# Hybrid attention block: where ScalarE's and VectorE's queued casts stand within a step

## The chip, the cores and the metric

One core of one Trainium2 chip runs the whole program. The metric is the device time of one execution in microseconds, the median over several runs. The work is shared by TensorE (PE, with its weight loads PEld), VectorE (DVE), ScalarE (ACT), GpSimd (POOL) and the DMA queue that SyncE (SP) issues to.

## What is computed

One layer over 1024 tokens of width 1024. Group A is neighbourhood attention on a 16 x 64 grid, group B windowed attention with rotary positions and a sink logit. Both have eight heads of 64 (group B two heads for keys and values).

```python
h = jnp.einsum('bsd,de->bse', x, w_in[layer])
q_a, k_a, v_a, z_a, q_b, k_b, v_b, z_b = jnp.split(h, SPLIT_POINTS, axis=-1)
y_a = neighborhood_attention(q_a, k_a, v_a, rel_pos_bias[layer])
y_b = windowed_gqa_with_sink(rotary(q_b), rotary(k_b), v_b, sink_logits[layer])
mixed = jnp.concatenate([y_a * jax.nn.silu(z_a), y_b * jax.nn.silu(z_b)], axis=-1)
y = jnp.einsum('bse,ed->bsd', mixed, w_out[layer])
x = layer_norm(DEEPNORM_ALPHA * x + y, ln_gain[layer], ln_bias[layer])
```

(The reshapes into heads are left out here.) The kernel keeps nearly full float32 accuracy by splitting operands into a high and a low float16 part, and multiplying high by high, high by low and low by high.

## The kernel before

The program has three parts. A prologue projects v in float32 and the first six of 21 tiles of 128 columns (`ORDER`, `NPRO`). Then comes a loop over attention units, and last `final()`: the rest of the output projection and the layer norm. The change lies in the loop (lines 1171 to 1240).

A **unit** is one head's block of 128 queries; there are 128 (`unit_list`: 64 of group B, then 64 of group A). At step i the loop issues the score matmuls of unit i (`stage_qk`, L815 and L816, into one of four "s" banks of PSUM), VectorE's fused reduction that adds the bias and finds the maximum (L825), ScalarE's exponential (`stage_exp`, L841), and for unit i-1 the split of the probabilities (`stage_tr`): high part on ScalarE (L851), low part on VectorE (L852), and a transposing DMA on SP (L855). The product with v follows for four units at once, at least six steps later (`stage_pv`, L880). It is then scaled (`stage_on`, L886 and L889), transposed (L900) and multiplied by the gate (L903, L909).

Between the score matmuls the loop fills TensorE with the **projection** of the remaining 15 tiles (`FILL`, `project`, L395), a tile being two halves of the tokens with 24 matmuls of 512 columns each, every half in one of two "pj" banks of PSUM. `FILL_AT` gives the steps over which a tile is spread, about eight for each. `pump_to(i + F1)` issues a first fifth of a step's share and `pump_to(i + 1)`, at the end of the step, the rest. When the 24th matmul is issued, `evac` queues what empties the bank. For k and q that is, for each of two heads on 64 partitions, a cast to the high part on ScalarE (L271, `hi` of `split_hl`) and a subtraction for the low part on VectorE (L277, `lo`). For gates z it is a tanh on ScalarE (L355) and a product on VectorE (L356). For rotary q it is a copy on ScalarE (L325), behind which a shuffle on VectorE and products on GpSimd follow. A bank can be written again only when all its readers are done, and with two banks that is one half (24 matmuls) later.

Each engine executes in the order of issue, which is written out by hand here: `enq` puts such an operation into a list of its engine with a priority (0 for those that hold a bank, 0.5 for weights, 1 for the rest), and `pop(eng, n, top)` issues up to n of those whose predecessors were issued in an earlier step, best priority first. In the loop before, `pop("dve", ...)` stands behind `stage_tr` and `stage_on`, then `stage_exp`, then `pop("act", ...)`, `pop("pool", ...)`, and the rest of the projection's share. So in a step ScalarE's order is L851 of the unit before, L841, queued operations; VectorE's is L825, L852 of the unit before, queued operations. `NA` and `ND` are 1: one queued operation for each engine and step; ScalarE gets two where its list holds five or more, or from step 105 on (`M_AT[0]`), VectorE two from step 112 on. `need` issues an operation at once where the order demands it.

Of the kernel before, what the change touches and what calls it, by code (L numbers as in the profile page):

```python
# [26 lines left out]
LTT, LPP, BP, BH, BR, ND, NA, NX, F1 = 1, 6, 2, 9, 5, 1, 1, 6, 0.2  # L27
# [18 lines left out]
M_AT = [105, 112, 118, 120]  # L46
# [16 lines left out]
def hybrid_block(ctx, tc, xT, x, wt, wv, wo, bias, sink, gain, lbias, cos, sin, bmask, out):  # L63
# [78 lines left out]
    queues = {e: [] for e in ENG}  # L142
    clock = {"step": None}
# [10 lines left out]
    def enq(eng, fn, *deps, prio=1, after=0):  # L154
        op = Op(eng, fn, deps, prio)
        if clock["step"] is not None:
            queues[eng].append(op)
        elif after:
            events.setdefault(ran[0] + after, []).append(op.emit)
        else:  # L160
            op.emit()
        return op

    ran, events = [0], {}

    def pop(eng, n, top=1):
        q = queues[eng]
        ready = [op for op in q if op.prio <= top and all(d.step is not None and d.step + d.lag < clock["step"] for d in op.deps)]
        for op in sorted(ready, key=lambda op: op.prio)[:n]:
            q.remove(op)  # L170
            op.emit()

    def need(*ops):
        for op in ops:
            if op.step is None:
                need(*op.deps)
                queues[op.eng].remove(op)
                op.emit()
# [244 lines left out]
    def wo_scan(n):  # L423
        nc.scalar.activation(scrap[:, :512], wo_raw[n], AF.Abs, accum_out=wom[:, n:n + 1])
# [310 lines left out]
    def gather_v(p, b):  # L735
        w = WINW[b]
        t = ap.tile([128, 4, 256], F16, tag="va", name=f"va{p}_{b}", bufs=6)
        bulk["last"] = bulk["step"]
        nc.sync.dma_start(t[:4 * w], vwin[b][p].rearrange("(g i) (c e) -> (i c) g e", g=4, e=256))
        va[p, b] = t  # L740
# [24 lines left out]
    def geom(u):  # L765
        g, p, j, t, _ = u
        if g == "a":
            b, half = t
            w = WINW[b]
            return NKEY[b], [4 * w] * 3  # L770
        lo, hi = max(t - 1, 0), min(t + 2, 8)
        return 128 * (hi - lo), [128] * (hi - lo)

    def stage_load(u, i):
        g, p, j, t, _ = u
        n, _c = geom(u)
        if g == "a":
            b, half = t
            if half == 0 and b != 2:
                bulk["last"] = clock["step"] + 1  # L780
                bt = ap.tile([128, 23 * WINW[1]], F32, tag="bs", name="bias", bufs=BR)
                o, m = BOFF[b], 23 * WINW[b]
                nc.sync.dma_start(bt[:, :m], bias[2 * p + j, :, o:o + m])
                bv = bt[:, :m]
                ld = Op("sp", None, [], 1)
                ld.step = i
                op = enq("pool", lambda: nc.gpsimd.tensor_scalar(bv, bv, rsg, -1.0, op0=ALU.mult, op1=ALU.mult),  # L787
                         ld, prio=0)
                st["bias"] = bt, op
            o = 11 * WINW[b] * half  # L790
            st[u, "b"] = st["bias"][0][:, o:o + NROW[half] * WINW[b]], st["bias"][1]
# [52 lines left out]
    def stage_tr(u):  # L844
        g, p, j, t, _ = u
        n, ch = geom(u)
        pt = st.pop((u, "p"))
        c, m = ch[0], len(ch)
        hl = split[units.index(u) % NSPLIT]
        src = pt[:, :n].rearrange("p (k c) -> p k c", c=c)  # L850
        nc.scalar.activation(hl[:, :m, 0, :c], src, AF.Copy, scale=PSCALE)  # L851
        nc.vector.scalar_tensor_tensor(hl[:, :m, 1, :c], src, PSCALE, hl[:, :m, 0, :c],  # L852
                                       op0=ALU.mult, op1=ALU.subtract)
        tr = ap.tile([128, 6, 128], F16, tag="tr", name="tr", bufs=BH)
        nc.sync.dma_start(tr[:, :2 * m, :], hl[:, :m].rearrange("p k i c -> p (k i c)"), transpose=True)  # L855
        st[u, "tr"] = tr

    def quad(q):
        g, p, j, t, _ = units[4 * q]
        return g, p, j, t // 4 if g == "b" else t[0] // 2  # L860
# [57 lines left out]
    def pump_to(u):  # L918
        n = 0
        for k, c in enumerate(FILL_N):  # L920
            u0, u1 = FILL_AT[k], FILL_AT[k + 1]
            n += int(c * min(max((u - u0) / (u1 - u0), 0), 1))
        pump(n - pumped[0])
        pumped[0] = max(n, pumped[0])
# [16 lines left out]
    def wo_max():  # L941
        nc.vector.tensor_reduce(wog, wom, axis=mybir.AxisListType.X, op=ALU.max)

    def wo_turn():
        ps = bank("t")
        nc.tensor.transpose(ps[:, :128], wog.to_broadcast([128, 128]), identf)
        wo_parts["max"] = ps
# [12 lines left out]
    def wo_load(n):  # L960
        if n < 16:
            tag = WO_TAG[n]
            pool, bufs = (rawp, 3) if tag == "raw" else (wp, {"wr": 5, "wor": 2}[tag])
            raw = pool.tile([128, 512], F32, tag=tag, name=f"wor{n}", bufs=bufs)
            e, a = WO_SEQ[n]
            nc.sync.dma_start(raw, wo[e, :, 512 * a:512 * a + 512])
            wo_raw[n] = raw
# [37 lines left out]
    def m_queue(e):  # L1005
        m_alloc(e, big)
        m_ops[e] = []
        for h in (slice(0, 512), slice(512, S)):
            o = enq("act", lambda h=h: nc.scalar.copy(mh[e][:, h], zt[e][:, h]))
            m_ops[e].append(enq("pool", lambda h=h: nc.gpsimd.tensor_sub(  # L1010
                ml[e][:, h], zt[e][:, h], mh[e][:, h]), o))
# [159 lines left out]
    for i in range(-LD, NU + LO):  # L1171
        if 0 <= i + LD < NU:
            stage_load(units[i + LD], i)
        if i < 0:
            continue
        clock["step"] = i
        per, h = divmod(i, 16)
        bulk["step"] = i
        if i in VA_AT:
            gather_v(0, VA_AT.index(i))  # L1180
        for n in range(len(WO_LD)):
            if WO_LD[n] == i:
                load_ops["wo", n] = enq("sp", lambda n=n: wo_load(n), wo_ops.get({9: 0, 10: 1, 12: 2, 13: 3}.get(n)),
                                        w_ops.get(17 + n if 4 <= n <= 8 else None))
                if n not in WO_PRE + WO_POST:
                    scan_ops.append(enq("act", lambda n=n: wo_scan(n), load_ops["wo", n]))
        if i == WO_MAX - 6:
            for n in WO_POST:
                scan_ops.append(enq("act", lambda n=n: wo_scan(n), load_ops["wo", n]))
        if i == WO_MAX:  # L1190
            need(*scan_ops)
            wo_max()
        for n in range(len(WO_AT)):
            if WO_AT[n] == i:
                wo_split(n)
        if i == 131:
            enq("sp", gain_load, *m_ops[4])
        if i in M_AT:
            m_queue(4 + M_AT.index(i))
        if bulk["last"] != i or (queues["sp"] and i - queues["sp"][0].born > 2):  # L1200
            pop("sp", 1 if i < 118 else 3)
        if i < NU:
            u = units[i]
            if u[3] in (0, 4):
                need(*stk_ops[f"b{u[1]}", u[2], u[3] // 4])
            if u[3] == (0, 0):
                need(*stk_ops[u[1], u[2], 0], *stk_ops[u[1], u[2], 1])
            stage_qk(u)
        q, m = divmod(i - LP - 3, 4)
        if i >= Q30 + 2:  # L1210
            q, m = (NU // 4 - 2, i - Q30 - 2) if i < Q30 + 4 else divmod(i - LP - 3, 4)
        elif i >= Q30:
            q, m = -1, 0
        if m == 0 and 0 <= q - 1 < NU // 4:
            stage_ot(q - 1)
        if m == 0 and 0 <= q < NU // 4:
            stage_pv(q)
        if i > Z3_END:
            pop("dve", 1, 0)
        if 0 <= i - LT < NU:  # L1220
            stage_tr(units[i - LT])
        if 2 <= i < 10:
            m_scale(i - 2)
        if i == WO_MAX + 3:
            wo_turn()
        if WO_MAX + 4 <= i < WO_MAX + 7:
            wo_scale(i - WO_MAX - 4)
        pump_to(i + F1)
        if 0 <= q < NU // 4:
            g, p, j, h = quad(q)  # L1230
            if g == "a" and p < 3 and (j, h, m) in VA_STEP:
                gather_v(p + 1, VA_STEP.index((j, h, m)))
        if m == 1 and 0 <= q < NU // 4:
            stage_on(q)
        pop("dve", ND if i < M_AT[1] else 2)
        if i < NU:
            stage_exp(units[i])
        pop("act", NA if i < M_AT[0] and len(queues["act"]) < 5 else 2)
        pop("pool", NP)
        pump_to(i + 1)  # L1240
    pump(10 ** 6)
# [77 lines left out]
```

## Time and profile before

| | us |
|---|---|
| median of 3 runs | 454.24 |
| lowest and highest | 451.89, 456.68 |
| the profiled execution | 452.2 |
| its span, first to last instruction | 450.4 |
| TensorE busy | 438.8 |
| VectorE busy | 347.1 |
| ScalarE busy | 300.9 |
| GpSimd busy | 231.9 |

The granted clock of TensorE is 0.994 of full speed over the span. A row of the profile gives line, engine, operation, what is written and read, and a count. In a row of the timeline the first number is the start and the second the time taken, both in us; a bracket says how long the engine stood idle before it and what ended that. In a row of waits stand the total in us, how often, and the longest. The modelled end of a matmul lies behind the start of the next, so that the distance between two starts tells more than a matmul's length.

### The profile page before, as it was taken

Reading aid. Unit: us, or ns where it says so; the run is one execution under the profiler, and the core shown is the slowest. Engines: PE = TensorE matmul, PEld = TensorE weight load, DVE = VectorE, ACT = ScalarE, POOL = GpSimd, SP = SyncE. Lnnn points to the kernel's source line nnn. Section 1 sums busy time; section 2 is a strip of 40 time slices with the busy share of each in tenths; the row PEclk is TensorE's granted clock in tenths of the full one; section 3 lists DMA queues with packets and bytes.
Section 4 is the critical chain, followed back from the end, with each engine's and each line's share of the span. In section 5 each row is a group of like instructions: output and inputs, shape, how many; then the busy total and the mean of one; then the engine's idle time right before and its main releaser. Section 6 shows DMA issues by size and latency. Waiting matters only on the chain.

```text
span 450.4 us, 9544 instructions
## 1 busy us (share of the span) xinstructions
PE 438.8 (97%) x3265; PEld 263.1 (58%) x3265; DVE 347.1 (77%) x860; ACT 300.9 (67%) x702; POOL 231.9 (51%) x246
## 2 busy tenths in 40 slices
PE   9999999999999999999999999999999999999992
PEld 8999974444445555555554565656546654444452
DVE  5878978839978787786788887887777847389954
ACT  5648659867588889888868877888678874012200
POOL 0003943555827849868506729755483547005741
PEclk9999999999999999999999999999999999999997
DMA  8898378977837889777979898989999989101711
GB/s 282 266 309 281 83 249 253 301 259 257 279 109 157 152 174 174 135 152 134 158 159 159 182 184 164 228 149 211 213 181 219 191 168 355 56 0 70 258 71 70
DMA packets 135280, 83.86 MB, mean 186 GB/s; under 512 B 101440, under 2 KB 113600, under 8 KB 134976
## 3 DMA queue, kind: packets, MB, share of 16 engines
q1 hardware_dynamic: 134800, 82.84, 75.3%
q8 instruction: 25, 0.41, 0.4%
q10 hardware_dynamic: 432, 0.43, 0.3%
q14 instruction: 23, 0.19, 0.1%
HBM read 52.83 MB, written 9.96 MB: 139 GB/s over the span
## 4 chain that ended last, share of the span: by engine, by line
PE 75%; DVE 7%; issue 7%; POOL 6%; ACT 3%; DMA 1%; DVEq 0%; SPq 0%; POOLq 0%; ACTq 0%
PE ps_pj L395 28%; PE ps_s L1028 9%; PE ps_t L880 6%; PE ps_s L476 6%; PE ps_pj L1028 5%; PE ps_t L1028 5%; PE ps_s L815 3%; PE ps_s L816 3%; PE ps_pj L476 3%; PE ps_t L476 3%; POOL wl L203 3%; POOL wr L202 2%; PE ps_t L900 2%; DVE split L852 1%; DVE sn L825 1%
## 5 line engine op out<-in xcount | busy, mean ns | idle before, releaser
L395 PE MATMUL ps_pj<-xf,wh 128*128 128x512 f16 x672 | 202.2, 379 | 1.8 <-DVE ks L277 1.1
L395 PE MATMUL ps_pj<-xf,wl 128*128 128x512 f16 x336 | 127.3, 379 | 0.0
L395 PEld LDWEIGHTS <-wh 128*128 128x128 f16 x672 | 63.5, 98 | 62.6 <-DVE ks L277 2.0
L852 DVE SCALAR_TENSOR_TENSOR split<-ps_s,split 128x384 f16<-128x384 f32 (+2 forms) x128 | 65.7, 514 | 33.1 <-ACT split L851 32.4
L841 ACT ACTIVATE ps_s<-sn,nm 128x385 f32<-128x385 f32 (+3 forms) x128 | 70.2, 548 | 29.0 <-DVE nm L825 27.2
L1028 PEld LDWEIGHTS <-m 128*128 128x128 f16 x408 | 39.7, 98 | 41.3
L851 ACT ACTIVATE split<-ps_s 128x384 f16<-128x384 f32 (+2 forms) x128 | 57.4, 448 | 1.8
L395 PEld LDWEIGHTS <-wl 128*128 128x128 f16 x336 | 32.9, 98 | 37.4
L202 POOL TENSOR_SCALAR wr<-wr,wsc 128x512 f32<-128x512 f32 x26 | 21.7, 836 | 42.9 <-ACT wh L197 37.9
L825 DVE CUSTOM_DVE_ANT_0 sn<-ps_s,bias,sg 128x264 f32<-128x264 f32 (+1 forms) x64 | 35.0, 547 | 8.3 <-PE ps_s L816 3.9
L825 DVE CUSTOM_DVE_ANT_0 sn<-ps_s,bm,nsk 128x384 f32<-128x384 f32 (+1 forms) x64 | 40.7, 636 | 0.6 <-PE ps_s L816 0.3
L1028 PE MATMUL ps_s<-wo,m 128*128 128x512 f16 (+1 forms) x192 | 40.7, 366 | 0.0
L815 PE MATMUL ps_s<-ks,qs 128*128 128x384 f16 (+4 forms) x128 | 39.2, 306 | 0.6 <-DVE zg L681 0.3
L816 PE MATMUL ps_s<-ks,qs 128*128 128x384 f16 (+4 forms) x128 | 39.2, 306 | 0.0
L787 POOL TENSOR_SCALAR bias<-bias,rsg 128x552 f32<-128x552 f32 (+1 forms) x24 | 18.6, 777 | 38.3 <-DMA bias<-in_bias 33.1
L880 PEld LDWEIGHTS <-tr 128*128 128x128 f16 (+1 forms) x1104 | 36.6, 98 | 2.2
L203 POOL TENSOR_TENSOR wl<-wr,wh 128x512 f16<-128x512 f32 x26 | 32.2, 1238 | 2.2
L1121 POOL TENSOR_TENSOR xr<-xr,gb 128x512 f32<-128x512 f32 x7 | 11.1, 1598 | 37.2 <-ACT xr L1118 37.2
L476 PE MATMUL ps_s<-wvh,x 128*128 128x320 f32 x128 | 29.5, 310 | 0.0
L309 POOL COPY ks<-ks 64x512 f16<-64x512 f16 x40 | 26.1, 660 | 6.2 <-DVE ks L279 1.8
L1028 PE MATMUL ps_pj<-wo,m 128*128 128x512 f16 (+1 forms) x120 | 26.4, 358 | 0.0
L524 POOL TENSOR_SCALAR xraw<-xraw,xsc 128x512 f32<-128x512 f32 x5 | 4.5, 905 | 39.2 <-ACT xf L522 39.2
(182 smaller groups left out, 826.8 us busy)
## 6 DMA issues: line engine op xcount, KB each, us to landing
xraw<-in_xT SPq DMA_DIRECT2D x31, 256.0 KB, 4.3
ws<-in_wt SPq DMA_DIRECT2D x15, 512.0 KB, 5.3
wr<-in_wt SPq DMA_DIRECT2D x26, 256.0 KB, 3.1
bias<-in_bias SPq DMA_DIRECT2D x16, 276.0 KB, 3.4
wor<-in_wo SPq DMA_DIRECT2D x16, 256.0 KB, 3.3
xr<-in_x SPq DMA_DIRECT2D x8, 512.0 KB, 9.1
out<-xr SPq DMA_DIRECT2D x14, 256.0 KB, 2.1
bias<-in_bias SPq DMA_DIRECT2D x8, 368.0 KB, 3.9
```

Of the source, the lines that this page charges most:

```text
L202: nc.gpsimd.tensor_scalar(raw, raw, scale, 1.0, op0=ALU.mult, op1=ALU.mult)
L203: nc.gpsimd.tensor_sub(l, raw, h)
L395: nc.tensor.matmul(ps, a[:, k % 4, :], mv, start=(k == 0 and i == 0), stop=(k == KT - 1 and i == 2))
L476: nc.tensor.matmul(ps[:, :320], lh[t // 4, k][:, ts], rh[k][:, cs], start=(k == 0 and i == 0), stop=(k == KT - 1 and i == 2))
L815: nc.tensor.matmul(ps[:, :m], q, sl[0], start=True, stop=False)
L816: nc.tensor.matmul(ps[:, :m], q, sl[1], start=False, stop=True)
L825: nc.vector.tensor_tensor_reduce(sn[:, :m], ps[:, :m], bias_t, sg[:, c:c + 1], init, op0=ALU.add, op1=ALU.min, accum_out=nm)
L841: nc.scalar.activation(pt[:, :m], sn[:, :m], AF.Exp, bias=nm, scale=-1.0, accum_out=sm[:, k:k + 1])
L851: nc.scalar.activation(hl[:, :m, 0, :c], src, AF.Copy, scale=PSCALE)
L852: nc.vector.scalar_tensor_tensor(hl[:, :m, 1, :c], src, PSCALE, hl[:, :m, 0, :c], op0=ALU.mult, op1=ALU.subtract)
L880: nc.tensor.matmul(ps[:, HD * m:HD * m + HD], a, b_, start=(i == 0), stop=(i == len(mms) - 1))
L1028: nc.tensor.matmul(ps, lh[:, ts], rh[:, cs], start=(e == EO[0] and i == 0), stop=(e == EO[-1] and i == 2))
```

## The change

Behind `stage_tr`, and so ahead of the exponential, one queued ScalarE operation of priority 0 may be issued; what it takes is subtracted from the step's number behind the exponential. `pop` now returns how many it issued, and takes `late`: with 1, predecessors issued in the same step count as done. If VectorE's list issued nothing in the step, one operation of priority 0 may be issued at the end of the step under that looser rule.

```diff
-    def pop(eng, n, top=1):
+    def pop(eng, n, top=1, late=0):
         q = queues[eng]
-        ready = [op for op in q if op.prio <= top and all(d.step is not None and d.step + d.lag < clock["step"] for d in op.deps)]
-        for op in sorted(ready, key=lambda op: op.prio)[:n]:
+        ready = [op for op in q if op.prio <= top and all(
+            d.step is not None and d.step + d.lag < clock["step"] + late for d in op.deps)]
+        ready = sorted(ready, key=lambda op: op.prio)[:n]
+        for op in ready:
             q.remove(op)
             op.emit()
+        return len(ready)
...
             stage_tr(units[i - LT])
+        early = pop("act", 1, 0)
         if 2 <= i < 10:
...
-        pop("dve", ND if i < M_AT[1] else 2)
+        turned = pop("dve", ND if i < M_AT[1] else 2)
         if i < NU:
             stage_exp(units[i])
-        pop("act", NA if i < M_AT[0] and len(queues["act"]) < 5 else 2)
+        pop("act", (NA if i < M_AT[0] and len(queues["act"]) < 5 else 2) - early)
+        if not turned:
+            pop("dve", 1, 0, 1)
         pop("pool", NP)
```

## The prediction

> **What bounds the kernel now.** I read the page first, then the busy times by stage, the waits of TensorE (its matmuls and its weight loads), the rows of TensorE in order of time, and last the rows of the two engines that the change reorders.
>
> ```profile
> span 450.4 us, 9544 instructions
> PE 438.8 (97%) x3265; PEld 263.1 (58%) x3265; DVE 347.1 (77%) x860; ACT 300.9 (67%) x702; POOL 231.9 (51%) x246
> 124.00:245.00 121.00, 120.35 (x1037) 67.88 (x1036) 97.64 (x290) 101.67 (x262) 74.04 (x76) 1.00 0.78 151
> ```
>
> TensorE is busy for 438.8 of 450.4 us. The third line is a stage of the loop, with the columns PE, PEld, DVE, ACT, POOL, granted clock: TensorE stands still for 0.65 of 121 us, and ScalarE (101.67, 84%) and VectorE (97.64, 81%) are full but not the bound. So an edit that only reorders casts can win no more than what TensorE waits for them. Those waits:
>
> ```profile
> PE ps_pj L395 <- DVE ks L277: 1.1, 1, 1.1
> PE ps_pj L395 <- DVE qs L277: 0.6, 1, 0.6
> PE ps_s L815 <- DVE zg L681: 0.3, 1, 0.3
> PE ps_s L815 <- DVE split L852: 0.2, 1, 0.2
> PEld L395 <- DVE ks L277: 2.0, 3, 1.4
> PEld L395 <- DVE qs L277: 1.2, 2, 0.8
> ACT qs L271 <- DVE qs L277: 5.5, 6, 1.2
> ```
>
> The reader should see that the low part of a k or q cast (L277) is the one thing of this change that TensorE waits for: 1.7 us by the matmuls' idle time, 3.2 us by the weight loads' (the two count the same waits and aren't added). The true loss lies between, because a matmul's modelled end hides part of a gap. It shows in the starts:
>
> ```profile
> 191.03 1.13 PE L880 MATMUL ps_t<-vb,tr 128*128 128x64 f16 x33
> 192.18 0.38 PE L395 MATMUL ps_pj<-xf,wh 128*128 128x512 f16 x1
> ...
> 229.09 1.13 PE L880 MATMUL ps_t<-vb,tr 128*128 128x64 f16 x33
> 230.21 0.38 PE L395 MATMUL ps_pj<-xf,wh 128*128 128x512 f16 x1
> ...
> 237.43 0.38 PE L395 MATMUL ps_pj<-xf,wl 128*128 128x512 f16 x1
> 237.85 0.38 PE L395 MATMUL ps_pj<-xf,wh 128*128 128x512 f16 x1
> ...
> 245.00 0.31 PE L815 MATMUL ps_s<-ks,qs 128*128 128x352 f16 x1
> 245.15 0.31 PE L816 MATMUL ps_s<-ks,qs 128*128 128x352 f16 x1
> 246.54 0.39 PE L395 MATMUL ps_pj<-xf,wh 128*128 128x512 f16 x1 [1.08 <-DVE ks L277]
> ...
> 275.41 1.22 PE L880 MATMUL ps_t<-va,tr 96*128 96x64 f16 x36
> 276.72 0.39 PE L395 MATMUL ps_pj<-xf,wh 128*128 128x512 f16 x1
> ...
> 335.69 0.28 PE L816 MATMUL ps_s<-ks,qs 128*128 128x264 f16 x1
> 336.53 0.39 PE L395 MATMUL ps_pj<-xf,wh 128*128 128x512 f16 x1 [0.56 <-DVE qs L277]
> ```
>
> L815 and L816 are alike, so their distance (0.15 at 245.00) is what such a matmul takes from start to start. From 245.15 the next should start at 245.30 and starts at 246.54: 1.24 lost. At 335.69 a matmul of 264 columns takes 0.11 (0.15 x 264 / 352), so 336.53 is 0.73 late. 512 columns take 0.22, so 237.85 is 0.20 late. The small matmuls L880 run at (1.13 - 0.19) / 32 = 0.03 each (0.19 being the modelled length of one), so 192.18, 230.21 and 276.72 are some 0.18, 0.15 and 0.25 late. **Sum 2.75 us**, between the two bounds.
>
> **The change part by part.** It adds and removes no instruction and no DMA. It moves two kinds: a high part, tanh or rotary copy that is ready (priority 0, L271, L355, L325) from behind the step's exponential (L841) to ahead of it on ScalarE, and the low part or product that follows (L277, L356) from the middle of the next step to the end of its own on VectorE, ahead of the next reduction (L825). One place, that of the largest stall, before the change (VectorE first, then ScalarE):
>
> ```profile
> 241.40 0.56 DVE L852 SCALAR_TENSOR_TENSOR split<-ps_s,split 128x384 f16<-128x384 f32 x1
> 241.87 0.17 DVE L886 RECIPROCAL ri<-sm 128x4 f32<-128x4 f32 x1
> 242.07 0.43 DVE L889 TENSOR_TENSOR on<-ps_t,ri 128x256 f32<-128x256 f32 x1
> 242.41 0.54 DVE L825 CUSTOM_DVE_ANT_0 sn<-ps_s,bm,nsk 128x256 f32<-128x256 f32 x1
> 243.06 0.56 DVE L852 SCALAR_TENSOR_TENSOR split<-ps_s,split 128x384 f16<-128x384 f32 x1
> 243.53 0.67 DVE L277 SCALAR_TENSOR_TENSOR ks<-ps_pj,ks 64x512 f16<-64x512 f32 x1
> 244.17 0.45 DVE L825 CUSTOM_DVE_ANT_0 sn<-ps_s,bias,sg 128x264 f32<-128x264 f32 x1
> 245.33 0.42 DVE L852 SCALAR_TENSOR_TENSOR split<-ps_s,split 128x256 f16<-128x256 f32 x1 [0.70 <-ACT split L851]
> 245.79 0.69 DVE L277 SCALAR_TENSOR_TENSOR ks<-ps_pj,ks 64x512 f16<-64x512 f32 x1
> ```
>
> ```profile
> 240.88 0.49 ACT L851 ACTIVATE split<-ps_s 128x384 f16<-128x384 f32 x1
> 241.47 0.59 ACT L841 ACTIVATE ps_s<-sn,nm 128x385 f32<-128x385 f32 x1
> 242.08 0.57 ACT L271 ACTIVATE ks<-ps_pj 64x512 f16<-64x512 f32 x1
> 242.56 0.47 ACT L851 ACTIVATE split<-ps_s 128x384 f16<-128x384 f32 x1
> 243.00 0.48 ACT L841 ACTIVATE ps_s<-sn,nm 128x257 f32<-128x257 f32 x1
> 244.30 0.59 ACT L271 ACTIVATE ks<-ps_pj 64x512 f16<-64x512 f32 x1 [0.70 <-DVE sn L822]
> 244.92 0.38 ACT L851 ACTIVATE split<-ps_s 128x256 f16<-128x256 f32 x1
> ```
>
> The bank's four readers go one after another: cast 242.08, low part 243.53, cast 244.30 (0.10 behind the low part's end; the profile names the short memset beside it), low part until 246.48, and 0.06 later TensorE starts. The bank's matmuls were issued by 237.43, so for over four us nothing but the order of the queues held the first cast back.
>
> I now lay the same durations in the new order. First cast behind L851: 241.37 to 241.94. (What is new is that the exponential now stands behind the cast's wait for the bank's last matmul; but that matmul stands ahead of the step's own score matmuls on TensorE, which the exponential needs anyway, so this wait costs it nothing.) Exponential 241.94, 0.47 later than before. VectorE ends L889 at 242.50, then takes the first low part until 243.17, then the reduction (242.41 before) until 243.71: **0.76 late**. L851 is ready at 242.65. The next L852 ends at 244.27 instead of 243.62: 0.65 late. The second cast goes behind L851 and the first low part, 243.2 to 243.8, without the wait of 0.70. Its exponential starts at 243.8, 0.8 late. The second low part, behind L852, ends at 244.95 instead of 246.48: **the bank is free 1.5 us earlier**, against a stall of 1.24. After that L851 (0.45 early) and the reduction after next (some 0.6 early) have won back the delay, since the wait of 0.70 on each of the two engines is gone.
>
> What covers the delay of 0.65 on L852: the score matmul four units on reuses its bank. For the L852 that ended at 243.62 that matmul is the one at 245.00, so 1.38 us of cover there, 0.7 left. With the cover gone it would cost up to 0.65 for each such pair of casts. SP's transposes wait for L852 and go as much later:
>
> ```profile
> DMA to landing us min/median/max: 2.4/3.2/5.6
> ```
>
> They land in a median of 3.2 us, and the matmuls that read them (L880) stand at least six steps behind in the program, so 0.65 lies inside that. POOL: copies of k (L309) become ready a step earlier, and have a priority below weights and bias, so nothing is moved behind them. On SP the order of issue stays as it is, since nothing that SP issues hangs on these casts.
>
> The tanh and its product (L355, L356) move in the same way, one pair for a bank. TensorE shows no wait for them: 0. The rotary copies (L325) move 0.6 within a step and have no low part behind them: 0, between -0.1 and +0.1 for each.
>
> Two edges. From step 105 on two ScalarE operations may go in a step: then the second cast stands behind the exponential, ahead of the first low part in the program. If the low part must wait for it, VectorE stands still for about one exponential, the next reduction comes some 0.8 late, and the bank is free about 1 us earlier instead of 1.5. That still covers the stall of 0.73. Also the test for five queued operations now sees one fewer: at exactly five, a cast of weights (L197) or a scan (L424) goes a step later. That is hidden by the eight or so steps for which weights are made ready ahead; a weight load that such a cast releases on SP goes a step later too, with the same cover.
>
> The first of these hangs on who may read a bank together. In the rows (5.5 us over six times in the waits of ScalarE on L277) the second cast waits for the first low part, though one reads partitions 64 to 127 and the other 0 to 63. The Trainium skill (PSUM — Partial Sum Buffer, section "PSUM bank collisions raise a hardware error") says that the compiler orders two engines on one bank, reads against reads too, but by quarters of the partitions, so that these two would be free. The trace differs: here the order goes by the whole bank. By that rule the sum would be the same at 2.75 and the delay of the edge 0 instead of 0.8, hidden either way.
>
> **Sum.** Gain at most 2.75 (the stalls), bounds 1.7 and 3.2. New waits: 0 where the cover holds as at the shown place; I take 0.15 for the first steps, where TensorE waits for the score banks already (0.3 and 0.2 in the waits), upper bound 11 (16 halves of k and q x 0.65). So 450.4 - 2.75 + 0.15 = 447.8 for the span and 449.6 for the profiled run (452.2). That run stands 2.0 under the median of 454.24; from the median the same 2.6 gives 451.6. I take the middle of the two bases, 450.6.
>
> **The rivals.**
> *The gain is lost at another wait* (no change). TensorE is then held up at the score banks or, at the loop's end, by SP, as much as it was at the projection's banks. For it: VectorE runs 81% full in the stage shown. Against it: the new order takes idle time out of both engines. Time: 452.2 on the profile's base, 454.2 on the median's. Chance 0.17.
>
> *The reductions come too late* (slower). Each low part now stands ahead of a reduction, so exponential, L852 and the score bank are late by 0.65 for each pair. Where the cover is smaller than that, TensorE waits. It decides as soon as the cover, 1.38 at the shown place, is under 0.65 at most pairs. 16 x 0.65 = 10.4 less 2.75 is +7.7: 460 to 462; with half of the pairs +2.5: 455 to 457. Against it: in the whole trace TensorE waits for L852 but once, 0.2. Chance 0.10, half of it with all pairs.
>
> *More than the stalls* (the shorter chain also removes the 0.3 and 0.2 at the score banks): 2.75 + 0.5 gives 449.0 to 451.0. Chance 0.08.
>
> **How the numbers follow.** The forecast, stalls gone and nothing new, has 0.65: 449 to 452 by its two bases. The range of 447.5 to 455.5 adds no change and the lighter half of the slower case above, and below the scatter of the runs (451.89 to 456.68 for one kernel). About 1% is what a measurement of this kernel can tell from no change. The forecast is 0.6%, so within 1% is likeliest, 0.70. Its distance to the bound is smaller than the scatter, and so faster by over 1% gets 0.20; slower by over 1% is the slower rival, 0.10.
>
> **What would show it.** Right: the waits of TensorE on L277 are gone, TensorE's busy time is the same 438.8 and its idle time some 2.7 less; in each pair the first cast starts behind L851 and ahead of L841; each low part ends 1.5 to 2 us earlier after its bank's last matmul; ScalarE's wait for L277 shrinks. Wrong: new waits of L815 on L852, or the waits of L825 and L841 growing by more than the casts' shrink; L880 late at the loop's end. The time itself would be wrong if the granted clock falls or if the stalls return at other banks.

## The result, and the profile after

| | before | after |
|---|---|---|
| median of 14 runs each, us | 452.75 | 450.8 |
| lowest and highest, us | 451.61, 456.68 | 450.17, 453.9 |
| span of the profiled execution, us | 450.4 | 448.4 |

The ratio of the times is 0.9961 [0.9943, 0.9978]: 0.4% faster, less than the 1% that separated "faster" from "the same". The forecast was 450.6. In spans the prediction said 2.6 less (447.8), and it became 2.0 less (448.4). The granted clock is 0.994 in both.

Span, busy times and the shown stage of the loop, from the page and the table by stage (columns PE, PEld, DVE, ACT, POOL, granted clock):

```profile
span 448.4 us, 9544 instructions
PE 438.1 (98%) x3265; PEld 263.4 (59%) x3265; DVE 347.2 (77%) x860; ACT 303.4 (68%) x702; POOL 231.2 (52%) x246
124.00:245.00 121.00, 120.72 (x1043) 68.16 (x1042) 99.85 (x295) 104.50 (x269) 75.48 (x78) 1.00 0.82 156
```

As many instructions, and the same work for TensorE (438.1 against 438.8). In the same 121 us TensorE gets six instructions further, VectorE five and ScalarE seven. Now the waits of TensorE in the loop:

```profile
PE ps_s L818 <- DVE qs L280: 0.7, 1, 0.7
PE ps_s L818 <- DVE zg L684: 0.3, 1, 0.3
```

(All lines behind the added ones are up by three: L395 is now L398, L271 and L277 are L274 and L280, L841 is L844.) The two waits of L395 on L277 are gone, and no matmul of the projection waits for a low part any more. In their place is one new wait, of a score matmul (L818) on a low part. The rows of the place of the largest stall, ScalarE, VectorE and TensorE in turn:

```profile
239.29 0.58 ACT L274 ACTIVATE ks<-ps_pj 64x512 f16<-64x512 f32 x1
239.77 0.57 ACT L844 ACTIVATE ps_s<-sn,nm 128x385 f32<-128x385 f32 x1
...
241.21 0.59 ACT L274 ACTIVATE ks<-ps_pj 64x512 f16<-64x512 f32 x1 [0.22 <-DVE ks L280]
```

```profile
240.45 0.67 DVE L280 SCALAR_TENSOR_TENSOR ks<-ps_pj,ks 64x512 f16<-64x512 f32 x1
241.04 0.53 DVE L828 CUSTOM_DVE_ANT_0 sn<-ps_s,bm,nsk 128x256 f32<-128x256 f32 x1
...
242.08 0.69 DVE L280 SCALAR_TENSOR_TENSOR ks<-ps_pj,ks 64x512 f16<-64x512 f32 x1
```

```profile
237.06 0.38 PE L398 MATMUL ps_pj<-xf,wl 128*128 128x512 f16 x1
...
244.58 0.31 PE L819 MATMUL ps_s<-ks,qs 128*128 128x352 f16 x1
244.73 0.59 PE L398 MATMUL ps_pj<-xf,wh 128*128 128x512 f16 x2
```

The first cast stands ahead of the exponential with 385 columns (239.77), the one that it stood behind before (241.47). The bank's last matmul starts at 237.06 and the last low part ends at 242.77: the bank is held 5.71 us, against 246.48 - 237.43 = 9.05 before. TensorE comes to it at 244.73, 1.96 us later, and 0.15 behind L819: it doesn't wait. The same count over all 16 halves of k and q: a bank was held for 6.0 to 9.7 us before and is held for 3.9 to 7.9 after. Before, eight of them came free only 0.05 or 0.06 us ahead of the next matmul; after, the least is 0.57 and the next 1.5. The other end of the account:

```profile
333.25 0.38 PE L398 MATMUL ps_pj<-xf,wl 128*128 128x512 f16 x1
...
334.34 0.59 PE L398 MATMUL ps_pj<-xf,wh 128*128 128x512 f16 x2
335.60 0.30 PE L818 MATMUL ps_s<-ks,qs 128*128 128x288 f16 x1 [0.66 <-DVE qs L280]
```

```profile
333.72 0.51 ACT L844 ACTIVATE ps_s<-sn,nm 128x288 f32<-128x288 f32 x1 [1.21 <-DVE nm L828]
334.16 0.19 ACT L844 ACTIVATION_READ_ACCUMULATOR ps_s<-sn,nm 128x1 f32 x1
334.25 0.57 ACT L274 ACTIVATE qs<-ps_pj 64x512 f16<-64x512 f32 x1
```

```profile
334.86 0.68 DVE L280 SCALAR_TENSOR_TENSOR qs<-ps_pj,qs 64x512 f16<-64x512 f32 x1 [0.80 <-ACT qs L274]
```

The tile q3 ends with the matmul at 333.25, and the score at 335.60 reads its second half. Two matmuls from 334.34 take 0.43, so the score is due at 334.77 and is 0.83 late. Before it are exponential, cast and low part, one behind the other. This is no bank that somebody holds but data that doesn't exist yet.

The balance of TensorE from start to start: 2.75 won at the projection's banks, 0.83 lost here, 1.92 in all against 2.0 in the spans. The rest cancels: the loop begins 0.38 later after a prologue that scatters, and a wait of 0.40 ahead of the score at 130.84 (before) is gone.

### The profile page after: what moved, and what is told of

It is laid out like the page before. It is cut to its first block, busy times and chain, and to the rows that moved or that the text cites. A ratio compares the mean times of both kernels' runs of the same rounds, so it can differ in the third digit from the quotient of the medians.

```text
span 448.4 us, 9544 instructions
## 1 busy us (share of the span) xinstructions
PE 438.1 (98%) x3265; PEld 263.4 (59%) x3265; DVE 347.2 (77%) x860; ACT 303.4 (68%) x702; POOL 231.2 (52%) x246
## 4 chain that ended last, share of the span: by engine, by line
PE 87%; DVE 4%; ACT 3%; DMA 3%; issue 1%; POOL 1%; DVEq 0%; POOLq 0%; ACTq 0%
PE ps_pj L398 40%; PE ps_s L1031 9%; PE ps_t L883 7%; PE ps_s L479 6%; PE ps_pj L1031 5%; PE ps_t L1031 5%; PE ps_s L818 4%; PE ps_s L819 3%; PE ps_pj L479 3%; PE ps_t L479 3%; DMA wos<-in_wo 2%; PE ps_t L903 1%; DVE sn L828 1%; ACT ps_s L844 1%; DMA xraw<-in_xT 1%
## 5 line engine op out<-in xcount | busy, mean ns | idle before, releaser
L398 PE MATMUL ps_pj<-xf,wh 128*128 128x512 f16 x672 | 202.2, 379 | 0.0
L398 PE MATMUL ps_pj<-xf,wl 128*128 128x512 f16 x336 | 127.5, 379 | 0.0
L398 PEld LDWEIGHTS <-wh 128*128 128x128 f16 x672 | 63.6, 98 | 59.7 <-issue 0.2
L844 ACT ACTIVATE ps_s<-sn,nm 128x385 f32<-128x385 f32 (+3 forms) x128 | 70.1, 548 | 27.1 <-DVE nm L828 25.9
L855 DVE SCALAR_TENSOR_TENSOR split<-ps_s,split 128x384 f16<-128x384 f32 (+2 forms) x128 | 65.6, 513 | 21.0 <-ACT split L854 20.2
L398 PEld LDWEIGHTS <-wl 128*128 128x128 f16 x336 | 32.8, 98 | 37.5
L828 DVE CUSTOM_DVE_ANT_0 sn<-ps_s,bias,sg 128x264 f32<-128x264 f32 (+1 forms) x64 | 35.2, 549 | 10.3 <-PE ps_s L819 4.8
L828 DVE CUSTOM_DVE_ANT_0 sn<-ps_s,bm,nsk 128x384 f32<-128x384 f32 (+1 forms) x64 | 40.7, 636 | 1.5 <-PE ps_s L819 1.3
L818 PE MATMUL ps_s<-ks,qs 128*128 128x384 f16 (+4 forms) x128 | 39.3, 307 | 0.9 <-DVE qs L280 0.7
L819 PE MATMUL ps_s<-ks,qs 128*128 128x384 f16 (+4 forms) x128 | 39.2, 307 | 0.0
L883 PEld LDWEIGHTS <-tr 128*128 128x128 f16 (+1 forms) x1104 | 36.6, 98 | 2.2
```

The source lines that it names most:

```text
L398: nc.tensor.matmul(ps, a[:, k % 4, :], mv, start=(k == 0 and i == 0), stop=(k == KT - 1 and i == 2))
L818: nc.tensor.matmul(ps[:, :m], q, sl[0], start=True, stop=False)
L819: nc.tensor.matmul(ps[:, :m], q, sl[1], start=False, stop=True)
L828: nc.vector.tensor_tensor_reduce(sn[:, :m], ps[:, :m], bias_t, sg[:, c:c + 1], init, op0=ALU.add, op1=ALU.min, accum_out=nm)
L844: nc.scalar.activation(pt[:, :m], sn[:, :m], AF.Exp, bias=nm, scale=-1.0, accum_out=sm[:, k:k + 1])
L883: nc.tensor.matmul(ps[:, HD * m:HD * m + HD], a, b_, start=(i == 0), stop=(i == len(mms) - 1))
```

## The experiments

Times are medians; each ratio is to the kernel before on the same chip, with its 95% interval. "The changed kernel" is the base of every edit except where another is named.

**Only the early cast.**

```diff
-        if not turned:
-            pop("dve", 1, 0, 1)
```

> Only the first half of the change: the cast goes ahead of the exponential, the low part stays in the middle of the next step. Theory (both halves are needed, since the bank's readers form one chain of cast, low part, cast, low part): laid out with the durations of the place at 241 us, a bank is free some 0.4 us earlier than before instead of 1.5, so the five small stalls go or shrink and of the one of 1.24 some 0.8 stays: 1.0 to 1.8 us under before, a ratio of 0.996 to 0.998. Rival 1 (the cast's place alone does it): as the whole change, 2.0 us under before and no wait of the projection on a low part. Rival 2 (the low part's place alone does it): as before, within 0.3 us.

450.58 us, 0.9941 [0.9914, 0.9969], span 448.8. The cast's place alone gives the whole gain. That both halves are needed is refuted. The theory gave 0.4 us for the place at 241; there the hold falls from 9.05 to 7.04. Banks are held for 5.3 to 8.7 us (3.9 to 7.9 with both halves), which is short enough for all of them but one:

```profile
PE ps_pj L398 <- DVE qs L280: 0.6, 1, 0.6
```

That one is q3's, 0.73 by the starts. The bank ahead of it comes free only 0.06 us before its next matmul, where the whole change leaves 0.57 at the least: the late half adds margin, but here no time. Here TensorE stands at q3's bank and the score just behind it finds its data; in the whole change it doesn't stand at the bank and then waits for the data. One takes the place of the other.

**Only the late low part.**

```diff
-        early = pop("act", 1, 0)
+        early = 0
```

> Only the second half: the cast stays behind the exponential, the low part may go at the end of the same step. Theory: VectorE then stands still for the exponential and the cast ahead of each low part, and the next reduction is some 1.4 us late; the bank is free some 0.7 us earlier than before. The small stalls go, 0.5 of the large one stays: 0.8 to 1.8 us under before, VectorE's wait for the cast (absent before, 3.6 us with the whole change) grows to 10 us or more. Rival 1 (the cast's place alone does it): as before within 0.3 us. Rival 2 (the low part's place alone does it): as the whole change, 2.0 us under before.

458.07 us, 1.0106 [1.0076, 1.0137], span 457.3: slower than before, which no theory had foreseen. VectorE's and ScalarE's waits:

```profile
DVE ks L280 <- ACT ks L274: 7.5, 10, 1.4
DVE z L359 <- ACT z L358: 7.5, 8, 1.7
DVE qs L280 <- ACT qs L274: 6.9, 11, 1.3
```

```profile
ACT ps_s L844 <- DVE nm L828: 40.4, 52, 1.7
```

With the cast still behind the exponential, the low part now stands at the end of the same step, and VectorE waits there for the casts of k and q (14.4 us, and 7.5 for the tanh of z) with the next reduction (L828) queued behind it. So the exponentials wait 40.4 us, against 25.9 in the changed kernel and 27.2 before. By the starts TensorE loses some 9.6 us in the loop (3.7 before), most of it at the projection's banks (3.2), the transposes (2.0) and the score banks (1.7). The late half does this harm only where the cast hasn't gone ahead.

**One step more for q3's low part.** The matmuls of q3 are spread over the steps from 105 to 111 instead of 112, so that the tile is done a step earlier, and the tile behind it begins there.

```diff
-FILL_AT = [... 97, 105, 112, 121, 123.5, ...]
+FILL_AT = [... 97, 105, 111, 121, 123.5, ...]
```

> The whole change, and the projection of q3 spread over six steps instead of seven, so that it ends a step before the first scores that read it. Theory (of the 2.75 us of stalls the last, 0.73, came back as a wait of the scores on the low part of the same q, 0.83): that wait goes, and the span is some 0.8 us shorter than with the change, 447.6. Rival (TensorE's remaining time is bound elsewhere, say by SP at the loop's end): the wait moves to another place and the span stays at 448.4 within 0.3.

453.6 us, 1.0002 [0.9974, 1.0029], span 451.6: the whole gain is lost.

```profile
PE ps_t L883 <- DMA tr<-split: 2.3, 2, 1.6
PE ps_s L818 <- DVE qs L280: 0.4, 1, 0.4
```

The score's wait shrinks only to 0.61 by the starts (0.4 idle), since the second cast now stands ahead of the first low part. And the product with v (L883) waits for transposes at 357 and 359: 0.86 and 1.77 by the starts. The wait goes to the end of the loop, as the rival said, and is larger there. The transpose of unit 115 starts 4.1 us behind the low part of its probabilities, 2.4 in the changed kernel.

**Every low part twice**, which holds the bank and VectorE 0.69 us longer, 32 times.

```diff
                 nc.vector.scalar_tensor_tensor(l(), src, QSCALE, h(), op0=ALU.mult, op1=ALU.subtract)
+                nc.vector.scalar_tensor_tensor(l(), src, QSCALE, h(), op0=ALU.mult, op1=ALU.subtract)
```

> The whole change with each of the 32 low parts of k and q executed twice (the same result written twice), 22 us more work for VectorE, ahead of the reductions. Theory (reductions have cover: banks have 1.5 us or more to spare with the change): TensorE waits little more, 0 to 2 us over the whole change. Rival (reductions ahead of which a low part stands are on the path): 16 pairs by 0.65 us or more, 8 us or more over the whole change.

470.65 us, 1.0374 [1.0342, 1.0405], span 469.3: 20.9 more than the changed kernel, for 32 x 0.69 = 22 us of work. Some 4.7 of it is a lower clock (0.984 over the span against 0.994, 1% of 469), the other 16.2 is waiting. The theory that cover swallows the added work falls: most steps have no 0.69 to spare.

**The same doubling in the kernel before** (the same added line, at L277).

> The kernel before the change with each of the 32 low parts of k and q executed twice, 22 us more for VectorE (the changed kernel paid 21 us in its span for the same). Theory (the loop of VectorE and ScalarE is as tight as TensorE, and extra work in it is paid almost one for one wherever it stands in the step): 20 to 28 us over before. Rival (the extra was dear because the change puts it ahead of the reductions): 5 to 12 us over before, from banks that are held longer.

474.91 us, 1.0489 [1.0475, 1.0503], span 473.0, 22.6 more than before (some 3.3 of it by the clock, 0.987). The waits are those of the banks, grown from 1.7 to 19.4:

```profile
PE ps_pj L396 <- DVE qs L278: 10.4, 7, 1.9
PE ps_pj L396 <- DVE ks L278: 9.0, 5, 2.5
```

The kernel before pays nearly all of it, too. With the work doubled, the change is worth 473.0 - 469.3 = 3.7 us: it makes a bank's evacuation begin earlier, and doesn't make it free.

**The same work without a bank.** Behind each low part stands an operation of the same size that reads and writes the low part itself and leaves it as it is.

```diff
+                nc.vector.scalar_tensor_tensor(l(), l(), 1.0, l(), op0=ALU.mult, op1=ALU.max)
```

> The whole change, with an extra VectorE operation of the same size behind each low part, which reads and writes the low part in SBUF only (its maximum with itself), so that it delays the next reduction as in the doubling, but holds no bank of the projection. Theory (the loop of VectorE and ScalarE is what the extra work lengthens): 12 to 22 us over the change, with waits of the scores on their banks and few on L280. Rival (in the doubling it was the bank being held longer): under 4 us over the change.

474.38 us, 1.0475 [1.0458, 1.0491], span 471.5, 23.1 more than the changed kernel (some 2.8 of it by the clock, 0.988). The added work itself holds no bank and costs as much. Three of TensorE's four largest waits, and ScalarE's largest:

```profile
PE ps_s L819 <- DVE split L856: 5.2, 10, 1.3
PE ps_pj L399 <- DVE qs L280: 3.8, 2, 2.0
PE ps_pj L399 <- DVE ks L280: 1.3, 2, 1.0
```

```profile
ACT ps_s L845 <- DVE nm L829: 49.7, 50, 1.9
```

The second and third row are banks of the projection all the same, 5.1 us: a second low part stands behind the added work of the first. So the run doesn't take these banks out of the account altogether: TensorE waits for them about as long as for the score banks. The exponentials' wait for their reductions goes from 25.9 to 49.7 us. The loop of reduction, exponential and split between VectorE and ScalarE is nearly as tight as TensorE. That VectorE is 81% full in the stage shown before the change doesn't mean that 19% is free: most of it, 19.7 of 23.4 us, is time in which it waits for ScalarE's splits (L851).

**q3 earlier, with one cast for a step.** The same 111, and ScalarE gets its second operation only from step 112 on.

```diff
-        pop("act", (NA if i < M_AT[0] and len(queues["act"]) < 5 else 2) - early)
+        pop("act", (NA if i < 112 and len(queues["act"]) < 5 else 2) - early)
```

> The whole change, q3 ending a step earlier as in the third experiment, and one queued operation for ScalarE until step 112 instead of 105, so that the second cast of q3 no longer stands ahead of the first low part. Theory (the score's wait of 0.61 that stayed was that second cast on the same bank; the 2.6 us of waits of the product with v on its transposes come from SP, which lags behind VectorE at the loop's end): the wait of the scores on q3 goes, the waits on the transposes stay or grow by the same 0.6, and the span stays at 451 to 452. Rival (the waits on the transposes come from ScalarE's order at step 111): they go too, and the span falls to 448 or less.

453.45 us, 1.0021 [1.0002, 1.0039], span 453.4. The score's wait on q3 is gone, so its cause is right. The transposes' wait stays, and something comes behind it. TensorE's rows, and the table by stage:

```profile
357.63 0.44 PE L883 MATMUL ps_t<-va,tr 96*128 96x64 f16 x9 [0.76 <-DMA tr<-split]
359.75 0.44 PE L883 MATMUL ps_t<-va,tr 96*128 96x64 f16 x9 [1.69 <-DMA tr<-split]
```

```profile
358.00:361.00 3.00, 1.31 (x16) 0.72 (x14) 0.56 (x1) 1.24 (x4) 0.00 (x0) 0.93 1.23 128
361.00:364.00 3.00, 3.00 (x10) 1.36 (x9) 1.84 (x6) 1.04 (x3) 0.00 (x0) 0.50 0.80 155
```

Behind the two waits the granted clock is 0.50 from 361 to 364, and a matmul takes twice as long. By the table that is 3 x 0.50 + 3 x 0.07 = 1.7 us on top of the waits (0.92 and 1.85 by the starts). This profile also loses 0.53 and 1.01 us at the start of the loop (125 and 132), which the changed kernel's doesn't; with a time of 455.23 it lies above the median.

**The gathers off SP.** As the one above, and for the last head pair the gathers of v are issued on ScalarE's queue.

```diff
-        nc.sync.dma_start(t[:4 * w], ...)
+        (nc.scalar if p == 3 else nc.sync).dma_start(t[:4 * w], ...)
```

> As the kernel with q3 ending early and its cast alone, and the four gathers of v of the last head pair issued by ScalarE instead of SP, which takes some 3 us of issue from SP between 333 and 347 us. Theory (SP's queue bounds the loop's end): SP's lag behind the low part falls by 1.5 us or more at units 114 to 120, the waits on the transposes shrink below 1 us, and the span is 447.5 to 449. Rival (the lag is the transposes' own rate): the lag and the waits stay, span 451 to 452. ScalarE may lose some 2 us of work time to the issues, which it would show as later exponentials.

450.51 us, 0.9943 [0.9929, 0.9956], span 449.4. No score waits for q3, and the wait for transposes is smaller:

```profile
PE ps_t L883 <- DMA tr<-split: 1.4, 2, 0.8
```

SP's rows at the same place of the changed kernel, then of this one:

```profile
346.29 1.32 SPq L742 DMA_DIRECT2D va<-vwin  x1
347.70 2.93 SPq L858 DMA_TRANSPOSE tr<-split  x2
```

```profile
344.02 0.57 SPq L969 DMA_DIRECT2D wor<-in_wo  x1
344.69 6.84 SPq L858 DMA_TRANSPOSE tr<-split  x3
```

The two in the changed kernel take SP's queue 1.6 and 1.2 us. Without the gathers between them three take 6.84, one of them 3.8. From issue to landing the transposes between 340 and 352 us take, in the changed kernel and then in this one:

```profile
DMA to landing us min/median/max: 3.0/4.0/5.9
DMA to landing us min/median/max: 3.1/6.4/8.2
```

SP's lag behind the low part is shorter up to unit 116 (1.6 us at unit 115 against 3.8 in the experiment above) and as long from 117 on (3.8 against 3.6). So SP's turn is only part of it: with the gathers elsewhere the transposes land later. What slows them there was not separated. The time is about that of the changed kernel, no better by the intervals.

**The last low part behind the first score.** Of the second half of a head's q the low part is issued behind that head's first score, not ahead. The line applies to every head of group A; q3 is the one that is meant.

```diff
-                need(*stk_ops[u[1], u[2], 0], *stk_ops[u[1], u[2], 1])
+                need(*stk_ops[u[1], u[2], 0], *stk_ops[u[1], u[2], 1][:-1])
...
+            if u[3] == (0, 0):
+                need(stk_ops[u[1], u[2], 1][-1])
```

> The whole change, and the first score matmul of a head pair issued ahead of the last low part of its q (it reads the first half of the tokens, that low part writes the second half). Nothing else moves. Theory (the 0.83 us wait of the scores on q3 is this dependency alone, and unlike the earlier ending of q3 this shifts no matmul work out of the loop's end): the wait goes, some 0.8 us less than the whole change, a span near 447.6 and a ratio to before near 0.994. Rival (the loop's end is bound by the transposes): the wait comes back as a wait of the product with v on its transposes, and the time is that of the whole change.

450.85 us, 0.9955 [0.994, 0.997], span 448.6. The wait of 0.83 stays:

```profile
PE ps_s L818 <- DVE qs L280: 0.7, 1, 0.7
```

The edit missed. The score that waits is the second one of the pair (288 columns), which truly reads the second half; the first (264 columns, at 333.47 in the changed kernel) never waited. This profile also has a wait of 0.89 by the starts at 125, of the projection for a product of z (L359). That of "q3 earlier, with one cast for a step" has one too (0.53), and so has the kernel before with doubled low parts (0.3 idle), so that it isn't put down to the change.

**The same edit with the early cast only.**

> The same edit on the first half of the change alone (cast ahead of the exponential, low part in the middle of the next step). Theory: the early cast is what frees the banks, so this is equal to the kernel with the whole change and the same edit, within 0.7 us, but for the 0.73 us that the projection waits at q3's bank there and that this edit does not remove: a span near 448.5. Rival (the low part at the end of the step has a gain of its own): 1 us or more slower than that kernel.

450.69 us, 0.9951 [0.9935, 0.9967], span 449.2. TensorE waits 0.73 at q3's bank and 0.16 at the score.

**The changed kernel again**, beside the last two.

> The whole change as it is, on the same chip and beside the same runs of before as the other two kernels of this call, so that they can be told apart: 0.996 of before, a span near 448.4.

450.66 us, 0.9953 [0.9934, 0.9972], span 448.8. The three are equal by their intervals: with the late half or without it, the time is the same.

**q3 earlier, the tile behind it at its place.** q3 is done by step 111, the next tile begins at 112 as in the changed kernel, and between them no projection is issued. ScalarE's second operation comes from 112 on, as in "q3 earlier, with one cast for a step" (the sixth experiment, as the text below counts).

```diff
-FILL_AT = [... 97, 105, 112, 121, 123.5, ...]
+FILL_AT = [... 97, 105, 111, 112, 121, 123.5, ...]
-    FILL_N = [48] * len(FILL) + [9, 9, 6, 12, 24]
+    FILL_N = [48] * (len(FILL) - 1) + [0, 48] + [9, 9, 6, 12, 24]
```

> The whole change, q3 ending a step earlier, its second cast not ahead of the first low part (as in the sixth experiment), but z3 begins where it did: one step has no projection, so that the loop's end keeps the matmuls which the earlier experiments took from it. Theory (the wait of 0.83 is a true dependency of the second score of the last head pair on the low part of q3's second half, and only the end of the loop, bound by the transposes, ate what its removal gave): the wait goes and the transposes lag no more than with the whole change, a span near 447.6 and a ratio near 0.994. Rival (the transposes bound the end anyway): the product with v waits for its transposes by about as much, 0.8 us, and the span stays at 448.4 to 448.8.

452.98 us, 0.9996 [0.9974, 1.0018], span 451.0: no faster than before. TensorE waits less for the transposes (0.42 by the starts), and the score at q3 still waits 0.57:

```profile
PE ps_s L818 <- DVE qs L280: 0.4, 1, 0.4
PE ps_t L883 <- DMA tr<-split: 0.3, 1, 0.3
```

Why the score waits here and not in "q3 earlier, with one cast for a step", the rows of the two tell. In both, the low part ends 1.9 us behind the start of the last score matmul of the unit before (334.74 to 336.68 there, 335.37 to 337.30 here), by way of the same reduction and split. But the empty step has no projection between that matmul and the next score, so that TensorE is due at the score that reads q3 after 1.42 us (336.79) and not after 2.29 (337.03). The edit took away the matmuls that had covered the low part.

The loop begins 1.5 us later in this profile than in that of the changed kernel, a wait of 0.40 comes at 374, in the output projection, and the loop's waits come to 0.8 more by the starts. That accounts for the profile's 2.6 us, but not for why the median of twelve runs is over 2 us above the change's. Neither theory gets it quite right. No kernel here beats the change by more than the intervals.

## Why the prediction was right, and where it was wrong

*The number.* The forecast of 450.6 against 450.8 is closer than the gain was: 2.6 us were forecast and the medians differ by 1.95. The forecast took a base of 453.2, the middle of a profile and a median of three runs; 14 runs give 452.75. The two errors nearly cancel, and that is luck. The range of 447.5 to 455.5 held no change as well as the gain, so that a time inside it says little; that the gain is real is said by the ratio's interval, which excludes no change. An effect of 0.4% can be told here, where the prediction took 1% for the least.

*What bounds the kernel.* Right. Only TensorE's waits at the projection's banks were to be had, 2.75 us from start to start, and 2.75 is gone. The rows of waits alone would have said 1.7 and 3.2; the distances between starts gave the number.

*The new order of the pair.* The place was right: cast ahead of the exponential, the second cast hardly waiting (0.22 in place of 0.70), and less waiting of ScalarE on low parts (5.5 us for q and 2.2 for k before):

```profile
ACT qs L274 <- DVE qs L280: 2.1, 5, 0.7
ACT ks L274 <- DVE ks L280: 1.6, 3, 0.8
```

The size was too small: the hold was to shrink by 1.5 and shrank by 9.05 - 5.71 = 3.3. Behind the bank's last matmul the same exponential stood at 241.47 - 237.43 = 4.04 before, and at 239.77 - 237.06 = 2.71 after, with the cast ahead of it. From that exponential to the bank's release the prediction laid out 244.95 - 241.94 = 3.01, and 242.77 - 239.77 = 3.00 was measured. So the layout itself held, and the whole difference of 1.8 us lies in where it began: it put the exponential 4.51 behind the bank's last matmul (241.94 - 237.43), and it stood 2.71 behind. The prediction laid out one place by itself and started it from the state of before. That idle time taken out of earlier steps had already brought the two engines forward fits this (with the early cast alone the same exponential stands 3.01 behind), but no run takes it apart. As the predicted 1.5 was already enough for the stall of 1.24, the sum didn't suffer.

*The edge of two casts in a step.* Right, by the whole bank. VectorE now waits for casts, three times out of four (1.40, 1.13 and 0.31) for the second one of a pair, ahead of the first low part. The row is the one of 1.13:

```profile
DVE qs L280 <- ACT qs L274: 1.9, 2, 1.1
DVE ks L280 <- ACT ks L274: 1.7, 2, 1.4
330.19 0.68 DVE L280 SCALAR_TENSOR_TENSOR qs<-ps_pj,qs 64x512 f16<-64x512 f32 x1 [1.13 <-ACT qs L274]
```

The fourth, 0.80, is the low part of q3 at 334.86, which waits for its own cast. The second cast and the first low part lie on different partitions of one bank, and write different tiles. By the rule of the Trainium skill that the prediction cites (PSUM — Partial Sum Buffer, section "PSUM bank collisions raise a hardware error"), the three waits for second casts wouldn't be there; the trace differs from it a second time.

*New waits, 0.15.* This is the term that was wrong. (Its upper bound of 11 is 10.4 by its own factors, 16 x 0.65.) "0 where the cover holds" looked at banks and at the score banks' reuse, and not at who reads the cast's result. The one wait that came, 0.83, is on q3's low part. The trace of before had it, in two rows that the prediction didn't look at, of TensorE and of VectorE:

```profile
337.62 0.29 PE L815 MATMUL ps_s<-ks,qs 128*128 128x288 f16 x1
```

```profile
335.78 1.46 DVE L277 SCALAR_TENSOR_TENSOR qs<-ps_pj,qs 64x512 f16<-64x512 f32 x2
```

The second of these two low parts, done at 337.24, is what the score reads. It started 0.38 later, and 0.73 of stall stood ahead of it. Without the stall it is due at 336.89 and waits 0.35, if the low part stays where it is. With 0.83 for 0.15 the sum would be 448.5 for the span; 448.4 was measured.

*The reason for 0 elsewhere.* The prediction gave two: a delay of 0.65 vanishes in 1.38 of cover, and the wait of 0.70 that goes on each engine wins the delay back. The doubled low parts and the added work without a bank show that work added to VectorE's loop is paid nearly in full (20.9 and 23.1 for 22 us; 16.2 and 20.3 without the clock's part). So cover alone, of which the added work finds little, isn't reason enough. What is left is the second: the change adds no work, and takes out more waiting (VectorE on the split L851 from 32.4 to 20.2 us) than it puts in. The number was right; that this is its reason is argued, and no run separates the two.

*Both halves.* The prediction moved low part and cast together and gave no value to each. The early cast alone gives 0.9941, the whole 0.9953 to 0.9961: the late half is worth nothing that these runs can tell, and the early cast is the cause of the gain.

*The rivals.* "The reductions come too late" didn't come with the whole change, but its mechanism is real: the late half alone is 1.1% slower through it. "The gain is lost at another wait" took 0.83 of 2.75; and SP at the loop's end, which it named, stood in the way of two attempts to get that back. Of "more than the stalls" nothing was seen beyond the scatter of the prologue.

*Left open.* What holds the transposes when SP's queue has fewer gathers, and why the last experiment's median is no better than before.

## What to carry to other kernels

Before you count a stall as won, take it out of the rows and look at the next instruction of that engine: which of its operands is just finished? Of a change with two halves, one can bring the whole gain and the other do harm by itself (the early cast alone 0.6% faster, the late low part alone 1.1% slower), so try the halves singly. And an engine that is 81% busy in a loop with another engine may have hardly any free time: add harmless work to it and measure what that costs.

## What the runs showed of the hardware

A short wait of TensorE can cost more than itself. In "q3 earlier, with one cast for a step", after 0.76 and 1.69 us of waits within 3 us (with 18 small matmuls between and behind), the granted clock was 0.50 for 3 us. With the low parts doubled in the changed kernel, one wait of 2.73 us had the same effect:

```profile
311.06 1.01 PE L399 MATMUL ps_pj<-xf,wh 128*128 128x512 f16 x2 [2.73 <-DVE qs L281]
```

```profile
311.00:315.00 4.00, 3.94 (x12) 1.60 (x12) 3.19 (x10) 3.30 (x8) 3.21 (x5) 0.57 0.74 79
```

In that stage the starts of matmuls of 512 columns lie 0.43 us apart, 0.22 elsewhere. But the length of a wait doesn't decide it alone. In "One step more for q3's low part" waits of 0.69 and 1.61 us at the same place left the clock at 1.00:

```profile
361.00:364.00 3.00, 3.00 (x17) 1.45 (x15) 2.28 (x8) 1.75 (x6) 0.00 (x0) 1.00 0.80 156
```

In the loop, over all profiles of this case, the four waits of 2.37 us and more were each followed within 1.4 us by a clock of 0.50. Of eleven between 1.6 and 2.3 us three were (1.69, 1.91 and 2.01) and eight weren't (1.61 to 2.22). What else decides, no run here shows.

The Trainium skill (TensorE: Matmul & The Clock Gate, section "HAM oscillation — how this bites in real kernels") gives idle gaps of over some 3.4 us as the rule. The trace agrees that waits halve the clock, but here gaps of 2.73 us, and of 1.69 with another shortly ahead, were enough. The waits of the change itself, 0.83 and less, left the clock at 1.00 where they stand.
